# Delta rule in an encoder kernel: group norm and splits on another engine, key tiles of one chunk

## Chip, cores and metric

The kernel runs on one core of a Trainium2 chip. The metric is the device time of one execution in microseconds (us). Engines are called as in the profile: PE (TensorE matmuls) and PEld (its weight loads), DVE (VectorE), ACT (ScalarE), POOL (GpSimd), SP (SyncE, which here only issues DMAs).

## The reference

Two encoder layers over 1040 tokens (16 meta tokens and 1024 tokens) of width 1024. Each layer has an input projection, four heads of latent attention, eight heads of a generalised delta rule that runs once forward and once backward over the tokens, an output projection with a layer norm, and a mixture of 32 experts. The change lies in the delta rule and in the output projection beside it:

```
sa = einsum('bhvk,bhk->bhv', S, kk_t)                       # one step of the scan
S  = S * w_t - sa * b_t + v_t * k_t ;  y_t = S r_t
...
y  = y_f + y_b                                              # both directions
yn = (y - mean) * rsqrt(var + eps) * gn_g + gn_b            # group norm, 64 channels a head
out = (yn + bonus) * g
mixed = concat([y_att, out]) @ w_out
```

The kernel does the scan in chunks of 64 tokens: inside a chunk a triangular system is solved with matrices, and a state of 64x64 a head goes from chunk to chunk.

## The kernel before, in words

Function `rwkv` holds the delta rule of a layer. 17 chunks and two directions give 34 steps (33 in the last layer), taken in turn: a step forward, a step backward. Two steps make a **job**. Four stages are called for a job, and the main loop (at the end of `rwkv`) calls them for different jobs: `chain` of job j, `levels` of job j+1, `grams` of job j+3, `blocks` of jobs j+2 and j+3 together every second time.

- `grams` (L1498) loads the keys of a job into tile `T` (SP, L1512) and their partners into `BK` (L1514, L1517), multiplies them (L1528, tile `e`), masks the result into the other half of `T` (DVE, L1533) and into `AA` (ACT L1534, POOL L1540), scales `BK` (ACT, L1543) and transposes it into `BT` (L1547, L1548).
- `blocks` (L1551) solves 16x16 blocks: three multiplications on POOL (L1560 to L1562) and then 45 short DVE instructions one behind the other (L1569 to L1571).
- `levels` (L1580) makes the inverses `Y` of 64x64 from these (PE L1597, L1602, L1611, L1618; POOL L1589; DVE L1587, L1603, L1604; ACT).
- `chain` (L1638) carries the state. For each step: `tu` = `T`·`ring` (L1659), ACT copies it (L1661), `tu` = `Y`·t (L1677), ACT writes it into `ring` (L1678, L1679), `st` = `BT`·`ring` (L1683), DVE adds the decayed state `sp` from POOL (L1673) and writes the next step's `ring` (L1686). The outputs go to PSUM tile `y` (L1666, L1690) and from there into `yt` (DVE L1693 or ACT L1695).
- `finish` (L1703) follows when both directions of a tile of 128 tokens are done, from the middle of the stage on: statistics on DVE and POOL (L1708 to L1716), loads of the bonus and the gate into `bg` (SP, L1718, L1719), transposes on PE into a PSUM bank (L1727), then scale and shift out of PSUM on ACT, four times 128 columns (L1730), and on POOL one addition of the bonus (L1731) and one multiplication by the gate (L1732) over 512 columns.
- `attended` (L950) is a generator that the main loop advances once or twice a job. It does the output projection in between: it splits activations into a high and a low part (`split`, L204: ACT writes the high one at L209, the low one is a subtraction at L212, here on POOL), and multiplies each tile in three matmuls (L201 to L203). First the attention's half (tile `yraw`), then the delta rule's (tile `yTr`) as `finish` delivers it.

Buffers: `T` lives in two pools, used by pairs of jobs, with two buffers each and a job (8 units of 2x128 columns) in a buffer; so four jobs of `T` are on the chip and a load for job j+3 goes into the buffer of job j-1. `BK` has two buffers, `ring` six, PSUM tiles `e` and `y` two each, `bg` one.

What sets the order: nothing is ordered by hand. The framework puts the instructions of every engine, and the DMAs of SP, in one order by its own estimate of when each could start, and each engine then takes them strictly in that order. So a change of an instruction or of a buffer's size also moves others.

Of the kernel before, what the change touches and what calls it, by code (L numbers as in the profile page):

```python
# [11 lines left out]
F32 = mybir.dt.float32  # L12
# [158 lines left out]
def hybrid_encoder(ctx: ExitStack, tc: tile.TileContext, I, out):  # L171
# [184 lines left out]
    for li in range(DEPTH):  # L356
# [594 lines left out]
        def attended(bank):  # L951


            for kc in range(4):
                w_out(kc)
            yield
            for i, n, col in TILES[:nt]:
                raw = fp.tile([128, 4, 128], F32, name="yraw")
                nc.sync.dma_start(raw[:, :, :n], yatt_d[:, :, col:col + n].rearrange("a p t -> p a t"))
                ya = pair(fp, [128, 4, 128], "ya")  # L960
                split(ya[:, :, :n], raw[:, :, :n], None, nc.gpsimd)
                ht = fp.tile([128, D], F32, name="ht", bufs=2)
                nc.sync.dma_start(ht[:n], h_rows[2 * li][row0(i):row0(i) + n])
                for j in range(2):
                    js = slice(j * 512, (j + 1) * 512)
                    ps = bank()
                    for kc in range(4):
                        mm3(ps[:n], ya[:, kc, :n], wo[kc][:, js], start=kc == 0, stop=kc == 3)
                    nc.vector.scalar_tensor_tensor(ht[:n, js], ht[:n, js], ALPHA, ps[:n], op0=OP.mult, op1=OP.add)
                    if j == 1:  # L970
                        nc.sync.dma_start(a_d[row0(i):row0(i) + n], ht[:n])
                    yield
            for kc in range(4, 8):
                w_out(kc)
            yield

            while True:
                if not ready:
                    yield
                    continue  # L980
                i = ready.pop(0)
                _, n, col = TILES[i]
                ya = pair(fp, [128, 4, 128], "ya")
                split(ya[:, :, :n], yTr[:, :, col:col + n], None, nc.gpsimd)
                ht = fp.tile([128, D], F32, name="ht", bufs=2)
                nc.sync.dma_start(ht[:n], a_d[row0(i):row0(i) + n])
                for j in range(2):
                    js = slice(j * 512, (j + 1) * 512)
                    ps = bank()
                    for kc in range(4):  # L990
                        mm3(ps[:n], ya[:, kc, :n], wo[4 + kc][:, js], start=kc == 0, stop=kc == 3)
                    nc.vector.scalar_tensor_tensor(ht[:n, js], ht[:n, js], 1.0, ps[:n], op0=OP.mult, op1=OP.add,
                                                   accum_out=sums[:n, i, j:j + 1])
                    if j == 1:
                        nc.sync.dma_start(a_d[row0(i):row0(i) + n], ht[:n])
                        done.append(i)
                    yield
# [470 lines left out]
def rwkv(tc, li, last, K, P, pc, kr_d, bk_d, bon_d, g_dram, vt_d, yT, mhalf, kept, side, ready):  # L1468
# [29 lines left out]
    def grams(runs, sv):  # L1498
# [1 line left out]

        U = 4 * sum(n for _, _, n in runs)

        T = sv[0].tile([128, U, 2, 128], F32, name="T")
        BK = kb.tile([128, U, 2, 64], F32, name="BK")

        at, u0 = [], 0
        for d, c0, n in runs:
            us = slice(u0, u0 + 4 * n)
            at += [(d, c0 + u // 4, u % 4) for u in range(4 * n)]
            u0 += 4 * n  # L1510
            for o, h in enumerate(HALF):
                nc.sync.dma_start(T[h, us, o], kr_d[d, h, c0:c0 + n].rearrange("p c i x -> p (c i) x"))  # L1512
            cs = bk_d[d, :, c0:c0 + n].rearrange("p c i (a t) -> p (c i) a t", a=2)
            nc.sync.dma_start(BK[lo, us], cs[lo])  # L1514
            for a in range(2):

                nc.sync.dma_start(BK[hi, us, 1 - a], cs[hi, :, a])  # L1517
        AA = sv[1].tile([128, U, 128], F32, name="AA")
        A, AR = AA[:, :, :64], AA[:, :, 64:]
        BT = sv[1].tile([128, U, 2, 64], F32, name="BT")  # L1520


        for q0 in range(0, U, 4):
            q = slice(q0, q0 + 4)
            ps = [pe.tile([128, 4, 128], F32, name="e") for _ in HALF]
            for u in range(4):
                for o, h in enumerate(HALF):
                    nc.tensor.matmul(ps[o][:, u], BK[h, q0 + u].rearrange("p a t -> p (a t)"), T[h, q0 + u, o],  # L1528
                                     start=True, stop=True)
            mask = K(f"mask{at[q0][0]}")  # L1530
            for o in range(2):
                a, b = HALF[o], HALF[1 - o]
                V.tensor_tensor(T[b, q, o], ps[o][b], mask[b, None, :].to_broadcast([64, 4, 128]), op=OP.mult)  # L1533
                nc.scalar.activation(AA[a, q], ps[o][a], AF.Copy)  # L1534
        u0 = 0
        for d, c0, n in runs:
# [7 lines left out]
        for q0 in range(0, U, 4):  # L1544
            ps = bank().rearrange("p (a b) -> p a b", a=4)
            for u in range(4):
                nc.tensor.transpose(ps[:, u], BK[:, q0 + u].rearrange("p a t -> p (a t)"), ident)  # L1547
            nc.scalar.activation(BT[:, q0:q0 + 4].rearrange("p u o x -> p u (o x)"), ps, AF.Copy)  # L1548
        return T, A, AR, BT, {x: u for u, x in enumerate(at)}

    def blocks(As, E):  # L1551
# [84 lines left out]
    shared = {}  # L1636

    def chain(job, s, Y):  # L1638
        T, _, AR, BT, units = s
        for d, c in job:  # L1640
            ring = rings.pop((d, c))
            x = steps.index((d, c))
            if x + AHEAD < len(steps):
# [5 lines left out]
            def un(i):  # L1649
                return units[d, c, i]  # L1650
# [5 lines left out]
            tu, ps = shared["tu"][:, x % 2], shared["st"][:, x % 2]  # L1656
            for i in range(4):
                for o in range(2):
                    nc.tensor.matmul(tu[HALF[o], i], T[:, un(i), o, 0:64], ring[:, i, o], start=True, stop=True)  # L1659
            t0 = ch.tile([128, 4, 64], F32, name="t0", bufs=2)  # L1660
            nc.scalar.activation(t0, tu, AF.Copy)  # L1661
            if want:
                py = pq.tile([128, 4, 64], F32, name="y", bufs=2)
                for i in range(4):
                    for o in range(2):
                        nc.tensor.matmul(py[HALF[o], i], T[:, un(i), o, 64:], ring[:, i, o], start=i == 0, stop=False,  # L1666
                                         skip_group_check=True)
            if more:
                nring = rings[d, orders[d][pos + 1]]
# [10 lines left out]
            if more:  # L1680
                for i in range(4):
                    for o in range(2):
                        nc.tensor.matmul(ps[HALF[o], i], BT[:, un(i), o], ring[:, i, o], start=True, stop=True)  # L1683
                for o in range(2):
                    a = HALF[o]
                    V.tensor_tensor(nring[a, :, o], ps[a], sp[a], op=OP.add)  # L1686
# [14 lines left out]
    def finish(cs, bank=bank):  # L1701
# [25 lines left out]
                        nc.tensor.matmul(ps[h, i, 64 * k:64 * k + 64], yt[h, c, i], ident[h, h], start=True, stop=True)  # L1727
        yn = yT[:, :, col:col + n]
        for i in range(4):
            nc.scalar.activation(yn[:, i], ps[:, i, :n], AF.Identity, bias=P("gnb", i), scale=P("gng", i))  # L1730
        nc.gpsimd.tensor_tensor(yn, yn, bg[:, 0, :, :n], op=OP.add)  # L1731
        nc.gpsimd.tensor_tensor(yn, yn, bg[:, 1, :, :n], op=OP.mult)  # L1732

    steps = [(d, orders[d][x]) for x in range(NC) for d in range(2) if x < len(orders[d])]
    cuts = [*range(0, len(steps), 2), len(steps)]
# [59 lines left out]
```

## Time and profile before

| what | value |
|---|---|
| three runs | 3145.37 us median, 3142.09 to 3153.57 |
| the profiled execution | 3157.96 us, span of its instructions 3156.2 us |
| PE busy | 2707.3 us, 86% of the span |
| PEld busy | 2209.1 us, 70% |
| DVE busy | 2165.3 us, 69% |
| ACT busy | 1650.5 us, 52% |
| POOL busy | 1050.7 us, 33% |
| mean granted TensorE clock | 0.888 of full speed |

The profiled execution is 12.6 us (0.4%) above the median of the runs. A row of the trace names the engine, the line of the kernel, the operation and the tiles (output<-inputs); "idle before" is the time in which the engine had nothing to do ahead of the instruction, and behind the arrow stands what ended it. The delta rule of the first layer lies from about 625 to 1130 us of the span, that of the second from about 2200 to 2715 us.

### The profile page before, as it was taken

The numbers are of one execution on the slowest core, as the hardware profiler recorded it, in microseconds if no ns is written. First come the engines' busy times: TensorE is split into PE (matmuls) and PEld (weight loads), VectorE is DVE, ScalarE is ACT, GpSimd is POOL, SyncE is SP. The second block draws the span as 40 slices with busy tenths as digits, with TensorE's granted clock in tenths as the row PEclk, the third lists the DMA queues.
The fourth block names the chain that finished last, engine by engine and source line by source line (L and its number), as shares of the span: only waits on it lengthen the run. The fifth ranks groups of instructions, "written<-read, shape, count | busy, mean of one in ns | idle before, by whom it ended". The sixth has DMA issues, their size and how long they took to land. (4 is left out here: it accounts for less than half of the span.)

```text
span 3156.2 us, 58039 instructions
## 1 busy us (share of the span) xinstructions
PE 2707.3 (86%) x22160; PEld 2209.1 (70%) x22160; DVE 2165.3 (69%) x4257; ACT 1650.5 (52%) x3604; POOL 1050.7 (33%) x1049
## 2 busy tenths in 40 slices
PE   5998799979999997999589997988799989799982
PEld 4888688768777775666388866877687777666661
DVE  7568655475766678989756756444667675789896
ACT  5434454444444447888543435434544453488882
POOL 3656211143334532121246631111433353321111
PEclk9999999978887897999789988998788879899996
DMA  5345610233322357999824465201433233699996
GB/s 175 97 137 185 205 48 21 75 93 102 94 68 78 108 198 259 358 360 352 303 91 137 155 194 186 65 21 51 107 108 101 69 93 100 214 333 356 352 347 244
DMA packets 342732, 523.77 MB, mean 166 GB/s; under 512 B 110732, under 2 KB 263308, under 8 KB 315808
## 3 DMA queue, kind: packets, MB, share of 16 engines
q1 hardware_dynamic: 234832, 399.11, 38.8%
q10 hardware_dynamic: 93280, 87.04, 8.1%
q0 software_dynamic: 14336, 33.84, 3.2%
q8 instruction: 176, 2.88, 0.4%
q14 instruction: 108, 0.88, 0.1%
HBM read 406.57 MB, written 129.84 MB: 170 GB/s over the span
## 5 line engine op out<-in xcount | busy, mean ns | idle before, releaser
L1221 DVE TENSOR_TENSOR w_lo<-raw,w_hi 128x512 fp32r<-128x512 f32 x768 | 481.7, 684 | 49.4 <-ACT w_hi L1217 49.1
L1217 ACT ACTIVATE w_hi<-raw 128x512 fp32r<-128x512 f32 x768 | 424.7, 625 | 71.0 <-DMA raw<-in_w_moe_dram 57.3
L201 PE MATMUL pj<-hT_hi,w_hi 128*128 128x352 f32 (+1 forms) x912 | 303.9, 334 | 3.0 <-ACT k L437 2.7
L202 PE MATMUL pj<-hT_lo,w_hi 128*128 128x352 f32 (+1 forms) x912 | 301.8, 331 | 2.8 <-DVE hT_lo L212 2.8
L203 PE MATMUL pj<-hT_hi,w_lo 128*128 128x352 f32 (+1 forms) x912 | 300.3, 330 | 0.0
L201 PE MATMUL ph<-w_hi,xT_hi 128*96 128x512 f32 x512 | 213.8, 418 | 3.9 <-ACT w_hi L1217 3.9
L202 PE MATMUL ph<-w_lo,xT_hi 128*96 128x512 f32 x512 | 206.0, 402 | 1.4 <-DVE w_lo L1221 1.4
L1458 POOL DMA_INDIRECT y_rows<-y,VS x64 | 59.9, 936 | 440.1 <-ACT y L1405 440.1
L1528 PE MATMUL e<-T,BK 64*128 64x128 f32 x1072 | 181.0, 352 | 28.5 <-DMA T<-kr_d 19.0
L203 PE MATMUL ph<-w_hi,xT_lo 128*96 128x512 f32 x512 | 205.3, 401 | 0.0
L212 DVE TENSOR_TENSOR pT_lo<-tr,pT_hi 128x512 fp32r<-128x512 f32 (+2 forms) x176 | 101.3, 592 | 130.1 <-ACT pT_hi L209 129.7
L201 PEld LDWEIGHTS pj<-hT_hi,w_hi 128*128 128x128 f32 x912 | 177.2, 195 | 13.3 <-issue 7.5
L1528 PEld LDWEIGHTS e<-T,BK 64*128 64x128 f32 x1072 | 152.7, 244 | 44.9 <-DMA T<-kr_d 15.6
L202 PEld LDWEIGHTS pj<-hT_lo,w_hi 128*128 128x128 f32 x912 | 176.8, 194 | 9.3 <-issue 4.9
L203 PEld LDWEIGHTS pj<-hT_hi,w_lo 128*128 128x128 f32 x912 | 176.4, 194 | 4.9 <-issue 4.3
L1533 DVE TENSOR_TENSOR T<-e,cc 64x512 f32<-64x512 f32 x134 | 92.2, 688 | 103.8 <-PE e L1528 101.2
L1673 POOL TENSOR_TENSOR sp<-ring,pc 64x256 f32<-64x256 f32 x126 | 84.7, 672 | 171.6 <-DVE ring L1686 150.8
L209 ACT ACTIVATE pT_hi<-tr 128x512 fp32r<-128x512 f32 (+2 forms) x176 | 87.0, 517 | 99.9 <-PE tr L873 98.3
L1277 POOL DMA_INDIRECT xs<-h_rows,XS x64 | 77.3, 1208 | 159.9 <-PE tp L1235 97.0
L1570 DVE TENSOR_TENSOR sb<-sb,dg 128x16 f32<-128x16 f32 (+8 forms) x270 | 106.5, 395 | 32.0 <-POOL dg L1562 24.8
L1540 POOL TENSOR_TENSOR AA<-AA,cc 128x256 f32<-128x256 f32 x67 | 52.0, 777 | 221.4 <-ACT AA L1534 161.8
L421 POOL TENSOR_SCALAR w_hi<-w_raw 128x1024 fp32r<-128x1024 f32 x34 | 102.3, 3010 | 59.4 <-PE pj L202 59.4
(422 smaller groups left out, 7678.3 us busy)
## 6 DMA issues: line engine op xcount, KB each, us to landing
raw<-in_w_moe_dram SPq DMA_DIRECT2D x192, 1024.0 KB
w_raw<-in_w_in_dram SPq DMA_DIRECT2D x38, 512.0 KB
T<-kr_d SPq DMA_DIRECT2D x134, 128.0 KB
ys<-y_rows SPq DMA_DIRECT2D x16, 1024.0 KB
a_d<-ht SPq DMA_DIRECT2D x25, 512.0 KB
h_rows<-h ACTq DMA_DIRECT2D x24, 512.0 KB
kr_d<-KR ACTq DMA_DIRECT2D x16, 576.0 KB
bk_d<-BK ACTq DMA_DIRECT2D x16, 576.0 KB
```

The costliest lines, as they stand in the source:

```text
L201: nc.tensor.matmul(o, a.hi, b.hi, start=start, stop=False)
L202: nc.tensor.matmul(o, a.hi, b.lo, start=False, stop=False)
L203: nc.tensor.matmul(o, a.lo, b.hi, start=False, stop=stop)
L209: hi = nc.scalar.activation(dst.hi, src, AF.Copy)
L212: return hi, e_lo.tensor_tensor(dst.lo, src, dst.hi.bitcast(F32), op=OP.subtract)
L421: nc.gpsimd.tensor_scalar(w.hi, wr, 1.0, None, op0=OP.mult)
L1217: nc.scalar.activation(w.hi[:, cs], raw[:, cs], AF.Copy)
L1221: V.tensor_tensor(w.lo[:, cs], raw[:, cs], w.hi[:, cs].bitcast(F32), op=OP.subtract)
L1528: nc.tensor.matmul(ps[o][:, u], BK[h, q0 + u].rearrange("p a t -> p (a t)"), T[h, q0 + u, o], start=True, stop=True)
L1533: V.tensor_tensor(T[b, q, o], ps[o][b], mask[b, None, :].to_broadcast([64, 4, 128]), op=OP.mult)
L1570: V.tensor_tensor(sb[:, :, cs], sb[:, :, cs], dg[:, :, t_:t_ + 1].to_broadcast([128, n, w]), op=OP.mult)
L1673: nc.gpsimd.tensor_tensor(sp[a], ring[a, :, o], pc[a, d, :, c:c + 1].to_broadcast([64, 4, 64]), op=OP.mult)
```

## The change

1. In `finish`, the scale by `gn_g` and the addition of the bonus are one DVE instruction for each 128 columns, which reads the sums from PSUM; the shift by `gn_b` and the multiplication by the gate are another. ACT's four instructions and POOL's two are gone.
2. In `attended`, the low part of the split of the activations is computed by DVE instead of POOL (the weights' split stays on POOL).
3. `T` holds one chunk of one direction (four units) with four buffers in each pool, and `BT` likewise. The bytes on the chip and the number of DMAs are the same.

```diff
-                split(ya[:, :, :n], raw[:, :, :n], None, nc.gpsimd)
+                split(ya[:, :, :n], raw[:, :, :n])
...
-                split(ya[:, :, :n], yTr[:, :, col:col + n], None, nc.gpsimd)
+                split(ya[:, :, :n], yTr[:, :, col:col + n])
...
-        T = sv[0].tile([128, U, 2, 128], F32, name="T")
+        T, BT = {}, {}
...
-            for o, h in enumerate(HALF):
-                nc.sync.dma_start(T[h, us, o], kr_d[d, h, c0:c0 + n].rearrange("p c i x -> p (c i) x"))
+            for c in range(c0, c0 + n):
+
+                T[d, c] = sv[0].tile([128, 4, 2, 128], F32, name="T", bufs=4)
+                for o, h in enumerate(HALF):
+                    nc.sync.dma_start(T[d, c][h, :, o], kr_d[d, h, c])
...
-        BT = sv[1].tile([128, U, 2, 64], F32, name="BT")
...
+            bt = BT[at[q0][:2]] = sv[1].tile([128, 4, 2, 64], F32, name="BT", bufs=4)
...
         for i in range(4):
-            nc.scalar.activation(yn[:, i], ps[:, i, :n], AF.Identity, bias=P("gnb", i), scale=P("gng", i))
-        nc.gpsimd.tensor_tensor(yn, yn, bg[:, 0, :, :n], op=OP.add)
-        nc.gpsimd.tensor_tensor(yn, yn, bg[:, 1, :, :n], op=OP.mult)
+            V.scalar_tensor_tensor(yn[:, i], ps[:, i, :n], P("gng", i), bg[:, 0, i, :n], op0=OP.mult, op1=OP.add)
+        for i in range(4):
+            V.scalar_tensor_tensor(yn[:, i], yn[:, i], P("gnb", i), bg[:, 1, i, :n], op0=OP.add, op1=OP.mult)
```

The instructions of the whole program: DVE gets 136 more in `finish` (128 of them of 128 columns, 8 of 16) and 28 splits (27 of 512 columns, one of 64), ACT loses 68, POOL loses 34 in `finish` and 28 splits. PE and SP have the same instructions as before, in another order. (The changed file's lines are 3 to 5 higher from `grams` on: L1528 is L1531 there, L1659 is L1664, L1677 is L1682, L1683 is L1688, L1686 is L1691, L1690 is L1695.)

The DMAs on SP's queue, in the middle of the first layer's stage, before:

```order
L1630 DMA ring<-vt_d 64x4x64 x2
L1512 DMA T<-kr_d 64x4x128 x4
L959 DMA yraw<-yatt_d 128x4x128
L963 DMA ht<-h_rows_103 128x1024
L1630 DMA ring<-vt_d 64x4x64 x2
```

and in the changed kernel:

```order
L1634 DMA ring<-vt_d 64x4x64 x2
L1515 DMA T<-kr_d 64x4x128 x2
L959 DMA yraw<-yatt_d 128x4x128
L963 DMA ht<-h_rows_103 128x1024
L1634 DMA ring<-vt_d 64x4x64 x2
L1515 DMA T<-kr_d 64x4x128 x2
```

The load of a job's keys came in one piece of four DMAs; now the first chunk's two come where the four were, and the second chunk's two behind the next load of `ring`.

PE around the second step of a job in the first layer, before (`tu<-t,Y` is a step's product with `Y`, `st` the new state, `e` the products of `grams` for a later job, `m<-X,AA` a part of `levels`):

```order
L1677 MATMUL tu<-t_6783,Y 64x64 x8
L1666 MATMUL y<-ring,T 64x64 x5
L1683 MATMUL st<-ring,BT 64x64
L1690 MATMUL y<-ring,AA 64x64
L1528 MATMUL e<-T,BK 128x128 x4
L1611 MATMUL m<-X,AA 32x32 x10
L1683 MATMUL st<-ring,BT 64x64 x7
```

and in the changed kernel:

```order
L1682 MATMUL tu<-t_6791,Y 64x64 x8
L1671 MATMUL y<-ring,T 64x64 x5
L1531 MATMUL e<-T,BK 128x128 x8
L1688 MATMUL st<-ring,BT 64x64
L1695 MATMUL y<-ring,AA 64x64
L1615 MATMUL m<-X,AA 32x32 x2
L1688 MATMUL st<-ring,BT 64x64 x7
```

The eight products of the first chunk's keys (4 of them behind the first `st` before, the rest later) now stand ahead of the second step's `st`. Leaving out one place with 40 at the start of the second layer, which both have, 49 such products stood between a step's `tu<-t,Y` and its `st`, in 12 places of the whole program; now 128 do, in 27 places.

DVE at one `finish` of the first layer, before (the scale, bonus and gate of `yTr` are on ACT and POOL):

```order
L1713 TENSOR_REDUCE gst<-gsq 128x8
L1571 TENSOR_TENSOR Y_10155<-Y_10155,sb 128x16x15
L1714 TENSOR_SCALAR gst<-gst 128x8
L1686 TENSOR_TENSOR ring<-st,sp 64x4x64 x2
L1577 TENSOR_TENSOR Y<-Y_10155,cc 128x512 x2
```

and in the changed kernel, at the same tile of attention outputs:

```order
L1735 SCALAR_TENSOR_TENSOR yTr<-m,cp,bg 128x128 x4
L1737 SCALAR_TENSOR_TENSOR yTr<-yTr,cp,bg 128x128 x4
L969 SCALAR_TENSOR_TENSOR ht<-ht,e 16x512
L212 TENSOR_TENSOR ya_lo<-yTr,ya_hi 128x512
L1691 TENSOR_TENSOR ring<-st,sp 64x4x64 x2
```

The eight new instructions and a split stand directly ahead of the additions that make the next `ring`.

## Rows read from the trace of the kernel before

**Rows 1.** Stretches: the two delta-rule stages without their starts; us busy (count), clock, DMA.
```profile
core 0: us, PE busy (x) PEld busy (x) DVE busy (x) ACT busy (x) POOL busy (x), PEclk, DMA share, GB/s
640.00:1120.00 480.00, 432.97 (x6067) 358.00 (x6068) 321.41 (x847) 210.58 (x485) 197.96 (x208) 0.80 0.33 94
2240.00:2720.00 480.00, 422.61 (x5942) 351.31 (x5943) 317.59 (x833) 208.53 (x481) 199.27 (x208) 0.82 0.37 110
```
**Rows 2.** PE's waits, 640 to 1120 us: total us, times, longest.
```profile
PE e L1528 <- DMA T<-kr_d: 9.2, 7, 2.8
PE e L1528 <- ACT AA L1534: 6.6, 8, 1.9
```
**Rows 3.** PE's waits, 2230 to 2720 us.
```profile
PE e L1528 <- DMA T<-kr_d: 9.7, 5, 2.2
PE y L1666 <- DVE yt L1693: 6.5, 2, 4.0
PE m L1611 <- DVE X L1604: 6.4, 6, 2.4
```
**Rows 4.** Timeline, second layer, SP and PE: start, us, engine, instruction, [idle before].
```profile
2570.58 1.91 SPq L1512 DMA_DIRECT2D T<-kr_d  x3
...
2574.06 1.26 PE L1528 MATMUL e<-T,BK 64*128 64x128 f32 x10 [2.20 <-DMA T<-kr_d]
...
2583.93 1.12 PE L1666 MATMUL y<-ring,T 128*64 128x64 f32 x16 [4.00 <-DVE yt L1693]
```
**Rows 5.** One stretch of 20 us behind it; columns as in Rows 1.
```profile
2580.00:2600.00 20.00, 13.03 (x182) 11.28 (x184) 14.17 (x38) 8.68 (x21) 6.95 (x7) 0.57 0.06 16
```
**Rows 6.** Instructions removed or moved: count, duration in ns min/median/max, first and last start.
```profile
L1730 ACT ACTIVATE yTr<-m,cp x56: 447/457/466, 965.3 to 2698.0; 128x128 f32<-128x128 f32 x56
L1731 POOL TENSOR_TENSOR yTr<-yTr,bg x17: 326/1281/2048, 966.9 to 2711.3; 128x512 f32<-128x512 f32 x16, 128x64 f32<-128x64 f32 x1
L1732 POOL TENSOR_TENSOR yTr<-yTr,bg x17: 320/1282/2156, 968.2 to 2712.7; 128x512 f32<-128x512 f32 x16, 128x64 f32<-128x64 f32 x1
...
L212 POOL TENSOR_TENSOR ya_lo<-yraw,ya_hi x17: 322/1272/1279, 683.5 to 2488.6; 128x512 fp32r<-128x512 f32 x16, 128x64 fp32r<-128x64 f32 x1
L212 POOL TENSOR_TENSOR ya_lo<-yTr,ya_hi x11: 1265/1277/1726, 1026.5 to 2679.5; 128x512 fp32r<-128x512 f32 x11
```
**Rows 7.** The like on DVE: a split, and an instruction of 128 columns with two inputs.
```profile
L212 DVE TENSOR_TENSOR yr_lo<-yTr,yr_hi x8: 218/680/693, 1122.4 to 2716.7; 128x512 fp32r<-128x512 f32 x7, 128x64 fp32r<-128x64 f32 x1
...
L1562 DVE TENSOR_TENSOR dg<-tmp x2: 283/288/292, 643.9 to 2225.1; 128x128 f32<-128x128 f32 x2
```
**Rows 8.** Groups by line, DVE, 640 to 1120 us: busy us, mean ns, idle before.
```profile
L1571 DVE TENSOR_TENSOR Y<-Y,sb 128x16 f32<-128x16 f32 (+9 forms) x135 | 54.3, 402 | 3.8
```
**Rows 9.** Timeline: DVE at L1710 alone, then beside a long POOL instruction; DVE at L1570 alone.
```profile
951.30 0.68 DVE L1710 TENSOR_TENSOR yt<-yt,gst 128x512 f32<-128x512 f32 x1
...
1023.96 2.57 POOL L212 TENSOR_TENSOR wo_lo<-ht,wo_hi 128x1024 fp32r<-128x1024 f32 x1
...
1024.24 2.84 DVE L1710 TENSOR_TENSOR yt<-yt,gst 128x512 f32<-128x512 f32 x1
...
2576.17 0.29 DVE L1570 TENSOR_TENSOR sb<-sb,dg 128x128 f32<-128x128 f32 x1
```
**Rows 10.** Timeline, first layer: POOL without a gap, and DVE behind it.
```profile
1026.50 1.73 POOL L212 TENSOR_TENSOR ya_lo<-yTr,ya_hi 128x512 fp32r<-128x512 f32 x1
...
1031.17 1.53 POOL L1731 TENSOR_TENSOR yTr<-yTr,bg 128x512 f32<-128x512 f32 x1
...
1048.23 0.19 DVE L1570 TENSOR_TENSOR sb<-sb,dg 128x16 f32<-128x16 f32 x1 [1.09 <-POOL dg L1562]
```
**Rows 11.** Timeline, end of the first layer's stage: two layer-norm instructions, and POOL beside them.
```profile
1134.91 3.52 DVE L228 SCALAR_TENSOR_TENSOR h<-hres,ln_st,l1b 128x1024 f32<-128x1024 f32 x2
...
1135.30 2.05 POOL L1731 TENSOR_TENSOR yTr<-yTr,bg 128x512 f32<-128x512 f32 x1
1137.42 2.16 POOL L1732 TENSOR_TENSOR yTr<-yTr,bg 128x512 f32<-128x512 f32 x1
```

More of the change, by code (lines that the diff above doesn't have):

```diff
@@ L1525, in grams @@
             ps = [pe.tile([128, 4, 128], F32, name="e") for _ in HALF]
+            Tq = T[at[q0][:2]]
             for u in range(4):
                 for o, h in enumerate(HALF):
-                    nc.tensor.matmul(ps[o][:, u], BK[h, q0 + u].rearrange("p a t -> p (a t)"), T[h, q0 + u, o],
+                    nc.tensor.matmul(ps[o][:, u], BK[h, q0 + u].rearrange("p a t -> p (a t)"), Tq[h, u, o],
                                      start=True, stop=True)
@@ L1532, in grams @@
                 a, b = HALF[o], HALF[1 - o]
-                V.tensor_tensor(T[b, q, o], ps[o][b], mask[b, None, :].to_broadcast([64, 4, 128]), op=OP.mult)
+                V.tensor_tensor(Tq[b, :, o], ps[o][b], mask[b, None, :].to_broadcast([64, 4, 128]), op=OP.mult)
                 nc.scalar.activation(AA[a, q], ps[o][a], AF.Copy)
@@ L1547, in grams @@
                 nc.tensor.transpose(ps[:, u], BK[:, q0 + u].rearrange("p a t -> p (a t)"), ident)
-            nc.scalar.activation(BT[:, q0:q0 + 4].rearrange("p u o x -> p u (o x)"), ps, AF.Copy)
+            bt = BT[at[q0][:2]] = sv[1].tile([128, 4, 2, 64], F32, name="BT", bufs=4)
+            nc.scalar.activation(bt.rearrange("p u o x -> p u (o x)"), ps, AF.Copy)
         return T, A, AR, BT, {x: u for u, x in enumerate(at)}
@@ L1638, in chain @@
     def chain(job, s, Y):
-        T, _, AR, BT, units = s
+        Ts, _, AR, BTs, units = s
         for d, c in job:
+            T, BT = Ts[d, c], BTs[d, c]
             ring = rings.pop((d, c))
@@ L1658, in chain @@
                 for o in range(2):
-                    nc.tensor.matmul(tu[HALF[o], i], T[:, un(i), o, 0:64], ring[:, i, o], start=True, stop=True)
+                    nc.tensor.matmul(tu[HALF[o], i], T[:, i, o, 0:64], ring[:, i, o], start=True, stop=True)
             t0 = ch.tile([128, 4, 64], F32, name="t0", bufs=2)
@@ L1665, in chain @@
                     for o in range(2):
-                        nc.tensor.matmul(py[HALF[o], i], T[:, un(i), o, 64:], ring[:, i, o], start=i == 0, stop=False,
+                        nc.tensor.matmul(py[HALF[o], i], T[:, i, o, 64:], ring[:, i, o], start=i == 0, stop=False,
                                          skip_group_check=True)
@@ L1682, in chain @@
                     for o in range(2):
-                        nc.tensor.matmul(ps[HALF[o], i], BT[:, un(i), o], ring[:, i, o], start=True, stop=True)
+                        nc.tensor.matmul(ps[HALF[o], i], BT[:, i, o], ring[:, i, o], start=True, stop=True)
                 for o in range(2):
```

## The prediction

> **What bounds the kernel now.** I read the busy time by stretches first, since only the delta rule's two stages are touched: 960 of 3156 us. In both, PE counts as busy for nine tenths of the time, but at a granted clock of 0.80 and 0.82 of full speed [rows 1]. So the stage is not at PE's peak: PE's order is a chain of short products with ACT and DVE between them, and where PE stands still the clock falls too. DVE is busy for 321 and 318 of the 480 us, POOL for 198 and 199, ACT for about 210 [rows 1]. Next I read PE's own waits, because in a stage bound by PE's order only they and the clock can be won. Keys that have not landed stand first: 9.2 us in seven waits in the first layer, 9.7 us in five in the second [rows 2, 3]. Behind these come waits for ACT (6.6 us, [rows 2]) and for DVE (6.5 and 6.4 us, [rows 3]). No wait of PE is ended by POOL in this list; POOL matters by what it does to DVE and by a place where it runs without a gap.
>
> **Keys in tiles of one chunk.** The load for job j+3 goes into the buffer of job j-1. As one tile it is free only when both steps of that job are done; as two tiles the first chunk's half is free a step earlier. The order shows that: the block of four DMAs becomes two and two, with `ring` between. The reader sees the price of the block in one place: the DMAs are issued at 2570.58 us, and PE stands for 2.20 us until 2574.06 us [rows 4]. Half of each load comes a step earlier, so I take off half of the 18.9 us of waits: **-9.5 us**; the ends are 0 (the second half waits as long as all did) and -18.9 (none is left). That place also shows what follows: after the 2.20 us and a second wait of 4.00 us [rows 4], the clock over the next 20 us is 0.57 and PE is busy for 13.03 us [rows 5]. At full clock this work takes 13.03 x 0.57 = 7.4 us. I count one such place: **-5.6 us**, say -6. Bounds for the clock in general: a hundredth of it over the 855.6 us of PE's busy time in both stages [rows 1] is 855.6 x 0.01 / 0.81 = 10.6 us. The new order could move it by two hundredths either way, so plus or minus 21 us.
>
> **Off POOL.** 34 instructions in `finish` (32 of 1.28 us, two of 0.32) and 28 splits (27 of 1.27, one of 0.32) go [rows 6]: 41.6 + 34.6 = about 76 us of POOL's 397. Nearly all of it was beside other work, since POOL idles for over half of the stage. On the path I put one place: in the first layer POOL runs without a gap from 1026 to 1048 us, with a split of 1.73, an addition of 1.53 and a multiplication of 1.28 us among the work [rows 6, 10], and behind it DVE waits for `blocks` [rows 10]. **-4.5 us**; ends 0 and -4.5, as DVE's own wait there was only 1.09 us and PE had other products.
>
> **Off ACT.** 64 instructions of 0.457 us and four shorter ones are 31 us of ACT's 419 [rows 1, 6]. What of ACT's time shows up as PE standing still: 6.6 of 210.6 us [rows 1, 2], or 3%. 3% of 31 us is **-1 us**; ends 0 and -31.
>
> **Onto DVE.** 27 splits of 0.68 us and 128 instructions of 128 columns with two inputs at 0.288 us [rows 7], the nine small ones at 0.2 us: 18.4 + 36.9 + 1.8 = 57 us. No row shows this form reading PSUM; `finish` takes a scalar and two tensors, and the nearest row is one with two tensors of the same size. Something comes back, because POOL slows DVE: the same L1710 takes 0.68 us alone and 2.84 us beside a POOL instruction of 2.57 us [rows 9]. Over the stage: L1571 has a mean of 402 ns [rows 8], while a middle size alone takes 0.29 us [rows 9]. That is 0.112 x 135 = 15 us of a layer, and its twin L1570, as many and of the same shapes, doubles it: 30 us for 198 us of POOL. The 76 us that POOL loses are then worth 11.5 us, and DVE's load grows by 57 - 11.5 = 46 us, from 639 to 685. Of DVE's time 6.5 + 6.4 us in 317.6 show up as PE standing still [rows 1, 3], 4%: **+2 us**. The lower end is -11.5 (only the relief counts), the upper end +57 (all of it on the path).
>
> The Trainium skill ("SBUF — State Buffer", § Who interferes with whom) says that DVE and GpSimd lock a shared port pair for a whole instruction, and that a DVE instruction takes part if it has two inputs in SBUF. The row of 2.84 us agrees. By this rule alone relief could be as much as the overlap, 76 us times DVE's busy share, some 50 us instead of 11.5, and DVE's term 0 instead of +2. The rule also speaks against a part of the change: the splits and the second instruction of each pair have two inputs in SBUF and enter the lock themselves, against the POOL work that stays. I leave the sum as the rows give it.
>
> **The stage's end.** The last tiles' `finish` runs beside the layer norm. POOL's two instructions take 2.05 and 2.16 us there, against 1.28 us elsewhere [rows 6, 11], and DVE's two beside them take 3.52 us together [rows 11]. With the pair on DVE (8 x 0.288 = 2.3 us) in place of 4.2 us on POOL I take 2 us off in each layer: **-4 us**; ends 0 and -5.
>
> **Sum**: -9.5 - 6 - 4.5 - 1 + 2 - 4 = -23 us. Against the profiled execution's 3158 us that is 3135; it is 12.6 us above the median of the runs, so against the median, which is what will be measured, 3145.4 - 23 = **3122 us**. About 0.5% (15.7 us) is what a measurement of this kernel can tell from no change.
>
> **Rivals.**
> - *The waits only move* (hidden anyway). The stage is a chain of in-order engines; keys that land earlier meet the next wait, on ACT or DVE, a microsecond later. For it: each T wait is short, and PE is busy for nine tenths. Against: 18.9 us is the largest item in PE's list. Then all terms are near 0: 3145 us.
> - *The clock rises.* For it: the clock of 0.57 stands right behind two waits of PE [rows 4, 5], so every wait that goes may give more than itself. Three hundredths more over both stages are 32 us: 3122 - 32 = 3090 us. Against it: a new order makes new waits, and the clock may as well fall.
> - *Products ahead of the state* (slower). In the new order 128 products of `grams` instead of 49 stand between a step's product with `Y` and its `st`, in 27 places instead of 12. PE takes them strictly in order, so if the first chunk's keys, now loaded just ahead of them, land late, the wait falls on the chain itself. Price: 27 waits of up to the 2.20 us seen [rows 4] are 59 us, in place of the 18.9 us of now; with the other four terms (-7.5 us) that is 3145 - 7.5 + 59 - 19 = 3178 us. It decides from the point where the keys land later than PE reaches the products; against it, in the trace only 12 waits for keys lie in 26 such loads, and half are loaded a step earlier than now.
> - *DVE becomes the bound* (slower). The new instructions stand ahead of the additions to `ring`; at 2583.93 us PE already waited 4.00 us because DVE was late [rows 4]. If the whole 46 us lie on the path and the other terms, without DVE's, hold (-25): 3145 + 46 - 25 = 3166 us. It decides where the products for `st` are done before DVE comes to the addition. Against it: DVE idles for a third of both stages.
>
> **How the numbers follow.** Forecast (3105 to 3140): 0.40. Waits only move: 0.24. Clock rises: 0.15. Products ahead of the state: 0.13. DVE the bound: 0.08. Faster by over 0.5% (below 3129.6) are three quarters and more of the forecast's cases, all of the clock's and a few of the moved waits': 0.32 + 0.15 + 0.02 = 0.49. Slower by over 0.5% (above 3161.1) are most of the two slower rivals: 0.19. Within 0.5%: 0.32. The range, 3088 to 3174 us, reaches from the clock's case to between the two slower ones and leaves out 2 in 10: the far ends of both.
>
> **What would show it.** Right: PE's waits for the keys fall from 18.9 us to about half; the two stages' POOL time falls by some 70 us and DVE's rises by 40 to 50; L1570, L1571 and L1710 get shorter; the layer norm's pair takes less than 3.52 us; both stages together are some 20 us shorter, and all other stages are as long as before. Wrong: waits for keys ahead of `st` that are as long as before or longer; a granted clock below 0.80 in the stages; waits of PE for the additions to `ring` and to `yt` of over 20 us (DVE the bound); or another stage's time moving by more than a few microseconds.

## The result, and the profile of the changed kernel

| kernel | median | runs | ratio to before |
|---|---|---|---|
| before | 3148.13 us | 3142.09 to 3153.57 (4) | 1 |
| changed | **3109.51 us** | 3103.86 to 3114.61 (4) | **0.9888**, 95% interval 0.9856 to 0.992 |

The change is worth 38.6 us between the medians, 1.1% by the ratio. The profiled execution of the changed kernel took 3103.86 us, 54.1 less than the one of before; 9.8 + 5.7 us of that are where the two profiled executions lie against the medians of the table. A second set of runs of the changed kernel, beside other kernels and with before on the same chip, gave 0.9887 (0.9846 to 0.9928).

The stretches of [rows 1], in the changed kernel:

```profile
core 0: us, PE busy (x) PEld busy (x) DVE busy (x) ACT busy (x) POOL busy (x), PEclk, DMA share, GB/s
640.00:1120.00 480.00, 421.44 (x6268) 347.10 (x6267) 361.39 (x977) 213.73 (x491) 174.12 (x188) 0.88 0.38 108
2240.00:2720.00 480.00, 419.08 (x5985) 345.69 (x5984) 352.72 (x1017) 211.24 (x496) 151.76 (x167) 0.87 0.39 119
```

The clock is 0.88 and 0.87 where it was 0.80 and 0.82. These windows now reach past the stage, so from here on a stage is cut where the chain begins and ends: from the first to the last copy of `t` by ACT (L1661, now L1666). Before:

```profile
670.20:1118.40 448.20, 412.60 (x5892) 340.00 (x5888) 297.67 (x775) 196.62 (x458) 182.37 (x191) 0.81 0.33 95
2256.20:2688.70 432.50, 395.91 (x5720) 329.19 (x5718) 283.25 (x760) 190.13 (x445) 176.12 (x186) 0.82 0.34 98
```

and changed:

```profile
675.00:1085.80 410.80, 369.21 (x5923) 304.45 (x5920) 311.75 (x843) 184.72 (x434) 150.02 (x165) 0.90 0.35 99
2220.30:2626.90 406.60, 369.43 (x5719) 305.99 (x5718) 296.12 (x824) 180.26 (x422) 140.69 (x160) 0.88 0.36 102
```

Such a row can be split into three parts: PE's idle time (length minus busy), the **loss to the clock** (busy x (1 - PEclk)) and the rest, which is the same work at full clock. Both stages together:

| | length | PE idle | loss to the clock | work at full clock |
|---|---|---|---|---|
| before | 880.7 | 72.2 | 149.7 | 658.9 |
| changed | 817.4 | 78.8 | 81.3 | 657.4 |

The work is the same, as it must be. PE stands still as long as before, 7 us longer even. In this pair of profiles the clock accounts for all of the 63 us of the two stages (PEclk is printed to two decimals, which leaves each loss open by some 4 us either way). The pair lies far apart, though: the mean granted clock of the whole execution is 0.888 and 0.908 in these two, but 0.893 on average over 27 executions of before and 0.899 over five of the changed kernel in the second set. So the table shows which kind of time went, and more of it than an ordinary pair of executions would. Of PE's waits, those for the keys, the largest item of [rows 2, 3] in each layer behind the wait for the first `ring` (10.4 and 17.7 us), are gone. PE's waits in the changed kernel, layer 1 (from 600 to 1130 us; columns as in [rows 2]):

```profile
PE tu L1664 <- DMA ring<-vt_d: 10.7, 1, 10.7
PE e L1531 <- ACT AA L1537: 6.4, 7, 2.0
PE m L1615 <- DVE X L1608: 5.5, 4, 2.6
PE st L1688 <- ACT ring L1683: 5.4, 5, 3.3
PE e L201 <- ACT AA L1537: 5.2, 5, 1.5
PE y L1671 <- DVE yt L1698: 5.1, 4, 3.0
```

and layer 2 (2150 to 2720 us):

```profile
PE tu L1664 <- DMA ring<-vt_d: 17.3, 1, 17.3
PE m L1615 <- DVE X L1608: 11.6, 4, 6.3
PE y L1671 <- DVE yt L1698: 9.8, 3, 6.7
...
PE e L1531 <- ACT AA L1537: 5.3, 7, 1.4
```

No row "T<-kr_d" is left, in either layer. In its place PE waits for DVE's `X` (11.6 us where [rows 3] has 6.4), for `yt` (9.8 for 6.5) and for ACT's `AA` and `ring`. The rest of the kernel did not stand quite still: from the first expert product of layer 1 to the first copy of `t` in layer 2 it takes 1042.9 us instead of 1050.8 (1043.7 in the second profile of the changed kernel).

DVE's rows that the change adds or that get shorter, over the whole kernel (columns: instructions | busy us, mean ns of one | idle before). Two of before:

```profile
L1571 DVE TENSOR_TENSOR Y<-Y,sb 128x16 f32<-128x16 f32 (+8 forms) x270 | 108.1, 401 | 7.5
L1570 DVE TENSOR_TENSOR sb<-sb,dg 128x16 f32<-128x16 f32 (+8 forms) x270 | 106.5, 395 | 32.0 <-POOL dg L1562 24.8
```

and of the changed kernel, where these two are L1575 and L1574:

```profile
L1574 DVE TENSOR_TENSOR sb<-sb,dg 128x16 f32<-128x16 f32 (+8 forms) x270 | 101.5, 376 | 20.7 <-POOL dg L1566 13.5
L1575 DVE TENSOR_TENSOR Y<-Y,sb 128x16 f32<-128x16 f32 (+8 forms) x270 | 97.6, 362 | 7.4
L1737 DVE SCALAR_TENSOR_TENSOR yTr<-yTr,cp,bg 128x128 f32<-128x128 f32 (+1 forms) x68 | 28.6, 476 | 0.1
L1735 DVE SCALAR_TENSOR_TENSOR yTr<-m,cp,bg 128x128 f32<-128x128 f32 x56 | 15.8, 344 | 22.8 <-PE m L1732 22.8
L212 DVE TENSOR_TENSOR ya_lo<-yraw,ya_hi 128x512 fp32r<-128x512 f32 (+1 forms) x17 | 11.9, 702 | 6.2 <-ACT ya_hi L209 6.2
L1715 DVE TENSOR_TENSOR yt<-yt,gst 128x512 f32<-128x512 f32 (+1 forms) x17 | 11.4, 671 | 0.3
```

With 9.0 us for the eleven splits of `yTr` and 2.9 us for the twelve L1735 at the stage's end, 68.2 us come onto DVE. Its busy time rises from 2165.3 to 2196.7 us only, by 31.4; POOL's falls from 1050.7 to 970.7, ACT's from 1650.5 to 1621.6.

### The profile page after: what moved, and what is told of

The parts are those of the page before. It is cut to its first block, busy times and chain, and to the rows that moved or that the text cites. A ratio compares the mean times of both kernels' runs of the same rounds, so it can differ in the third digit from the quotient of the medians.

```text
span 3102.0 us, 58102 instructions
## 1 busy us (share of the span) xinstructions
PE 2640.3 (85%) x22160; PEld 2152.1 (69%) x22160; DVE 2196.7 (71%) x4421; ACT 1621.6 (52%) x3536; POOL 970.7 (31%) x987
## 5 line engine op out<-in xcount | busy, mean ns | idle before, releaser
L1221 DVE TENSOR_TENSOR w_lo<-raw,w_hi 128x512 fp32r<-128x512 f32 x768 | 482.1, 684 | 48.7 <-ACT w_hi L1217 47.5
L1531 PE MATMUL e<-T,BK 64*128 64x128 f32 x1072 | 152.3, 316 | 13.3 <-ACT AA L1537 11.7
L1531 PEld LDWEIGHTS e<-T,BK 64*128 64x128 f32 x1072 | 126.6, 211 | 28.2 <-ACT AA L1537 15.2
L1277 POOL DMA_INDIRECT xs<-h_rows,XS x64 | 76.2, 1191 | 160.9 <-PE tp L1235 89.1
L226 POOL TENSOR_TENSOR ln_st<-ln_st,mhalf 128x1 f32<-128x1 f32 (+1 forms) x43 | 66.1, 1538 | 168.6 <-DVE ln_st L225 152.7
L201 PE MATMUL o<-pT_hi,V_hi 128*128 128x256 f32 (+3 forms) x288 | 95.2, 331 | 26.7 <-ACT yatt L881 26.7
```

What stands on the lines that cost most here:

```text
L201: nc.tensor.matmul(o, a.hi, b.hi, start=start, stop=False)
L1221: V.tensor_tensor(w.lo[:, cs], raw[:, cs], w.hi[:, cs].bitcast(F32), op=OP.subtract)
L1277: return nc.gpsimd.indirect_dma_start(out=x, out_offset=None, in_=src[:], in_offset=bass.IndirectOffsetOnAxis(ap=xi, axis=0), bounds_check ...
```

## The experiments

Two theories stood against each other after the result: the parts act by what they take away (keys that come late, POOL and ACT), or the framework's new order of all engines carries the gain and the parts are the occasion. Each kernel was timed against before on the same chip; the ratio is to that.

**The parts alone.** Each kernel is before with some of the diff's hunks and nothing else.

Key tiles of one chunk (the hunks in `grams` and `chain`):

> Only the key tiles of one chunk (T and BT per chunk); the splits and the group norm stay where they were. Theory A, the key tiles carry the gain: PE's waits of the e products for T (18.9 us over both layers before, none in the changed kernel) are gone here too, the granted clock of the two stages rises from .80 and .82 to .86 or more, and the time is 3105 to 3122 us (ratio .987 to .992). Theory B, the moves from POOL and ACT to DVE carry it: the key waits go, but the clock stays near .81 to .83 and the time is 3130 to 3148 us. Theory C, the parts are worth what the prediction gave them (keys 15.5 of 23 us): scaled to the measured 39 us, some 26 us here, 3122 us, with the clock about two thirds of the way up.

Both moves to DVE (the hunks in `attended` and `finish`):

> Only the moves to DVE (the group norm's sums from PSUM and the splits of ya); keys in whole-job tiles as before. Theory A: the waits for T stay (some 15 to 19 us over both layers), the clock stays at .80 to .83, the time is 3138 to 3150 us. Theory B: most of the gain is here, 3105 to 3125 us, with the clock at .86 or more though the key waits stay. Theory C: some 13 us, 3135 us. In every theory POOL's busy time falls by about 76 to 80 us and DVE's rises by 30 to 50.

Only the hunk in `finish`:

> Only the group norm's affine part and its sums on DVE, with operands taken from PSUM; splits on POOL, keys in whole-job tiles. Theory A: 3138 to 3155 us. Theory B: half or more of what both moves bring. As the eight instructions of 128 columns took 343 ns each in the changed kernel and not 288, DVE's busy time should rise by some 45 us less relief from POOL; ACT's falls by some 29 us. If the end of the stage is what the DVE copies lengthen (last step to first expert product +5 us in the changed kernel), that stretch is 83 us in layer 1 and 70 in layer 2 here too.

Only the two hunks in `attended`:

> Only the splits of ya on DVE instead of POOL (28 of 1.28 us off POOL, .68 us on DVE); group norm and keys as before. Theory A: 3138 to 3150 us, within half a per cent of before. Theory B: the split ahead of the output product is half a microsecond shorter in 28 places and POOL is 36 us freer; at most 15 us, 3133 us. If the end of the stage is lengthened by the group norm alone, the last step to the first expert product is 76 to 78 us in layer 1 here, as before or shorter.

| kernel | ratio (95% interval) | key waits, both layers | PE idle | loss to the clock | work |
|---|---|---|---|---|---|
| key tiles | 0.9936 (0.9913 to 0.9958) | 0 | 91.4 | 106.1 | 651.6 |
| both moves | 0.9966 (0.9939 to 0.9993) | 11.7 | 85.4 | 98.4 | 659.1 |
| norm only | 1.0066 (1.0028 to 1.0104) | 23.0 | 96.3 | 144.1 | 656.8 |
| splits only | 1.0013 (0.9988 to 1.0037) | 14.0 | 79.0 | 107.6 | 661.4 |

The key tiles bring 20 us and both moves 11: by size this is theory C, the shares that the prediction gave them. The clock of the stages rises with either part alone (to 0.86 and 0.86, and to 0.88 and 0.86), where theories A and B each expected it to stay low with one of them. But the two halves of the moves don't add up: the norm alone costs 21 us, the splits alone nothing, both together gain. A sum of separate effects on the engines does not give that. The row of the splits alone also shows what a loss read from one profile is worth: it is 42 us below that of before, and the time is the same. POOL's busy time is as expected in all of them: 1048.9 us with the key tiles, which take nothing off it, and 971.2, 1005.1 and 1013.1 in the other three. That the norm lengthens the stage's end is not shown either: the stretch from the last copy of `t` to the first split of an expert weight on DVE (L1221, 8 to 10 us ahead of the first expert product itself) is 81.1 us in layer 1 with the norm alone and 84.0 with the splits alone.

**A new order and nothing else.**

```diff
-            for o, h in enumerate(HALF):
+            for o, h in reversed(list(enumerate(HALF))):
                 nc.sync.dma_start(T[h, us, o], kr_d[d, h, c0:c0 + n].rearrange("p c i x -> p (c i) x"))
```

> The kernel before, with the two key loads of a run issued in the other order (upper half first): nothing is added or moved between engines, but the framework's order of all engines is drawn anew. Theory O, a new order alone moves the time by as much as the parts of the change did: at least 8 us from before, either way. Theory P, the parts act by what they take from an engine or free in a buffer: within 5 us of before (3143 to 3153 us), with the key waits at 15 to 22 us over both layers. In both theories the decomposition should hold: stage time = work at full clock (668 to 680 us for both stages in the six kernels so far) + PE's idle time + half of the time at the lower clock level.

Measured: 3137.54 us where before took 3163.52 on this chip, ratio **0.9922** (0.9892 to 0.9953). No work moved, no buffer changed, and 25 us are gone: as much as the key tiles bring (20 us), within the two intervals. Its stages:

```profile
674.40:1102.40 428.00, 379.28 (x5890) 311.09 (x5887) 295.99 (x775) 193.12 (x459) 181.88 (x191) 0.87 0.35 99
2236.70:2651.30 414.60, 361.88 (x5718) 299.21 (x5718) 276.86 (x759) 187.36 (x445) 174.48 (x186) 0.89 0.35 101
```

PE idle 101.4 us, loss to the clock 89.1, work 652.0. Two of its waits, layer 1 and layer 2:

```profile
PE e L1528 <- DMA T<-kr_d: 1.1, 2, 0.8
...
PE e L1528 <- DMA T<-kr_d: 1.3, 2, 0.9
```

So the waits for keys, 18.9 us before, can go with whole-job tiles too. A new order alone moves the time by more than the 8 us that theory O asks for. It does not rule theory P out: that forecast holds only while the key waits stay at 15 to 22 us, and they fell to 2.4. Over the five kernels with whole-job tiles the ratio even goes nearly in step with the key waits: 0.9922 at 2.4 us, 0.9966 at 11.7, 1.0013 at 14.0, 1 at 18.9, 1.0066 at 23.0, about 2 us of time for each us of waits. Whether late keys cost that much, or whatever else an order brings makes both, no run separates.

**Keys held back.** The changed kernel with `name="T", bufs=3` instead of 4:

> The changed kernel with three instead of four buffers for the key tiles of one chunk: a key load has to wait for a step that comes later. Theory P: waits for keys come back (over 10 us in both layers together, none before), the time at the lower clock level rises from 218 us towards 280 or more, and the time is 3125 to 3145 us. Theory O: the time is anywhere from 3100 to 3150 us and bears no relation to the key waits.

Measured: 3445.6 us, ratio 1.0894 (1.0858 to 1.0931), outside of both theories. The first stage:

```profile
677.70:1257.70 580.00, 443.76 (x5982) 369.70 (x5978) 297.81 (x837) 189.97 (x443) 144.20 (x167) 0.74 0.25 70
```

Over both stages PE idles 279.9 us and loses 226.9 to the clock. Of its waits in layer 1, PE's and SP's queue:

```profile
PE m L1601 <- DVE X L1591: 45.8, 7, 10.8
PE e L1531 <- DMA T<-kr_d: 22.0, 8, 3.1
...
SPq L1634 <- PE y L1695: 186.1, 23, 26.5
```

Keys are late again (45.2 us in both layers), but the larger part is elsewhere: SP waits 186.1 us to load the next steps' `ring` (29.6 in the changed kernel) and PE waits for the inverse. Which of the two comes first is not settled. What the fourth buffer saves is far more than the waits that name the keys.

**The start of the stage filled.** In the main function, behind the first `ring` tiles of the changed kernel (the products are not read by anyone):

```diff
                 new_ring(*steps[x])
+            for _ in range(2):
+                pf = bank()
+                for x in range(6):
+                    nc.tensor.matmul(pf.rearrange("p (a b) -> p a b", a=8), ident, gs[0][1], start=True, stop=True)
```

> The changed kernel with twelve products of 128x512 (identity times the first job's AA, into a bank that nobody reads) in PE's queue just ahead of the first product with the state, where PE waits 10.7 us in layer 1 and 17.3 in layer 2 and the clock is at its lower level for some 40 us of the next 45. Theory C, PE's standing still is paid for through the clock: the fill keeps the level up, about half of 40 us comes back in each layer, less up to 3 us where the fill is longer than the wait: 3075 to 3100 us. Rival: the low level there has another cause (the short dependent products behind the wait), the stretches stay, and the time is 3108 to 3125 us.

Measured: ratio 0.9929 (0.9903 to 0.9955), so no gain over 0.9888; applied to before's 3148 us it is 3126 us, just above both ranges. Layer 1 from 655 to 700 us, the changed kernel and then the filled one:

```profile
655.00:700.00 45.00, 27.26 (x228) 23.73 (x228) 33.02 (x85) 17.96 (x37) 26.85 (x27) 0.55 0.52 138
```

```profile
655.00:700.00 45.00, 32.77 (x286) 23.48 (x285) 31.02 (x70) 18.12 (x40) 24.26 (x26) 0.73 0.52 135
```

The lift of the clock is there: the wait for `ring` falls from 10.7 to 3.1 us and the clock rises from 0.55 to 0.73. The gain is not: the first copy of `t` comes at 686.4 us, not earlier than the 675.0 and 680.9 us of the two profiles of the changed kernel. ACT's rows show what it stands behind, in the changed kernel and then in the filled one:

```profile
674.02 1.06 ACT L209 ACTIVATE wo_hi<-ht 128x1024 fp32r<-128x1024 f32 x1 [12.61 <-DMA ht<-in_w_out_dram]
674.98 0.37 ACT L1666 ACTIVATE t<-tu 128x256 f32<-128x256 f32 x1
```

```profile
684.66 0.63 ACT L209 ACTIVATE ya_hi<-yraw 128x512 fp32r<-128x512 f32 x1 [4.05 <-DMA yraw<-yatt_d]
685.20 1.26 ACT L1546 ACTIVATE BK<-BK,pc 128x128 f32<-128x128 f32 x4
686.36 0.36 ACT L1666 ACTIVATE t<-tu 128x256 f32<-128x256 f32 x1
```

In both, PE's sixteen products for `tu` are done a microsecond or two (at 673.0 and 682.6 us) before ACT leaves its wait for a load of the output projection, and the copy comes behind that. So in layer 1 PE's pace does not set that time; in layer 2 of the changed kernel the copy waits 0.9 us for PE. The fill also drew a new order: ten of the sixteen products run at 669.95 us, and the other six come from 681.90 us on, behind products of `grams` and `levels` for which PE waits 2.35 and 4.00 us. What the lifted clock would be worth in the old order, and behind this place, the run does not show.

**The stage's end.** The changed kernel, but the tiles that are finished after the last step keep ACT and POOL:

```diff
+        if at_end:
+            for i in range(4):
+                nc.scalar.activation(yn[:, i], ps[:, i, :n], AF.Identity, bias=P("gnb", i), scale=P("gng", i))
+            nc.gpsimd.tensor_tensor(yn, yn, bg[:, 0, :, :n], op=OP.add)
+            nc.gpsimd.tensor_tensor(yn, yn, bg[:, 1, :, :n], op=OP.mult)
+        else:
...
```

> The changed kernel, but the tiles that are finished after the last step, beside the layer norm, keep ACT's scale and shift and POOL's addition and multiplication. If DVE's eight instructions there are what makes the stretch from the last step to the first expert product 83.5 and 70.1 us long (78.3 and 65.3 before), it falls by some 5 us in each layer: 3100 us. If it is the splits and the order, it stays: 3105 to 3115 us. By theory O the order of both stages is drawn anew too, and the time may move by 10 us or more either way.

Measured: 0.9898 (0.9862 to 0.9935), the changed kernel's ratio. The stretch from the last copy of `t` to L1221 is 85.6 and 68.1 us, as in the changed kernel (83.5 and 70.1): DVE's instructions there are not what lengthens it.

**Where the wide products lie.** Three more kernels test whether the clock follows the 128x512 products of `attended` that stand between the chain's short ones; the changed kernel runs beside them.

> The changed kernel once more, as it stands, as the anchor for the three runs beside it. Every theory: the ratio to before is .985 to .992. Its granted clock in the two stages is .86 to .89 and the time lost to the clock (PE's busy time, each microsecond weighted with what the granted clock lacks to full speed) about 84 us over both stages, as in the first profile of it (before: 160).

```diff
-        for _ in range(2 if j < 5 else 1):
+        for _ in range(1 + (j % 2 == 0)):
```

> The changed kernel with the output projection's generator advanced twice in every other job and once in the others, instead of twice in the first five jobs and once after that: the 128x512 products lie more evenly. Theory W, the clock of a stretch follows how much 128x512 work lies in it: in the eighths of the stage that hold 28 or more us of it the clock takes 0 to 7 us, in those that hold under 16 it takes 7 to 14 (before). An even spread then loses less: 60 to 80 us instead of 84, and the time is 10 to 25 us below the changed kernel beside it. Theory O, it is a new order and no more: within 15 us of it, either way.

```diff
             stage(k, x)
-        for _ in range(2 if j < 5 else 1):
-            next(side)
+            if k == 3 or (k == 0 and j < 5):
+                next(side)
```

> The changed kernel with the generator advanced as often as before, but between the stages of a job (behind the chain and behind the key products) instead of behind all four: the number per job is the same, only the emission order differs. Theory W: little changes in how the 128x512 work is spread over the stage, so within 6 us of the changed kernel beside it. Theory O: 10 us or more away from it, either way, though nothing is added, removed or moved to another engine.

```diff
-        for _ in range(2 if j < 5 else 1):
+        for _ in range(4 if j < 5 else 1):
```

> The changed kernel with the generator advanced four times instead of twice in the first five jobs: the attention's half of the output projection is done by the fifth job, and the middle of each stage has no 128x512 work until the first tiles are finished. The work is the same. Theory W: the middle of each stage (some 100 us) falls to the lower clock level for most of its time, the loss to the clock rises by 20 to 50 us in all, and the time is 20 to 60 us above the changed kernel beside it. Theory O or a stage bound by its waits: within 15 us of it.

| kernel | ratio (95% interval) | PE idle | loss to the clock | work |
|---|---|---|---|---|
| changed, again | 0.9887 (0.9846 to 0.9928) | 74.4 | 101.8 | 652.3 |
| every other job twice | 0.9982 (0.9951 to 1.0012) | 90.8 | 91.3 | 669.3 |
| between the stages of a job | 0.9947 (0.9924 to 0.9971) | 91.5 | 90.1 | 660.7 |
| four in the first five jobs | 1.0046 (1.0022 to 1.007) | 116.7 | 127.4 | 644.0 |

The changed kernel again has its ratio, but a loss of 101.8 us where some 84 were expected. The bunched kernel went as theory W has it, 1.6% (45 us) above the changed one, with 26 us more loss. Its middle, where no 128x512 product is left (855 to 975 us), and the same stretch of the changed kernel (second profile, 860 to 980):

```profile
855.00:915.00 60.00, 47.56 (x818) 41.08 (x816) 39.28 (x127) 25.89 (x64) 18.16 (x24) 0.77 0.25 66
915.00:975.00 60.00, 40.97 (x706) 35.11 (x706) 39.15 (x116) 22.63 (x55) 16.91 (x22) 0.72 0.20 52
```

```profile
860.00:920.00 60.00, 56.13 (x1034) 47.52 (x1034) 43.32 (x116) 31.99 (x77) 24.10 (x30) 0.97 0.33 90
920.00:980.00 60.00, 50.10 (x836) 40.69 (x834) 57.07 (x171) 23.93 (x57) 21.04 (x23) 0.86 0.33 90
```

Without wide products both PE's busy time and the clock fall. But spreading them more evenly than the changed kernel does lost 0.95% (20 us between the medians) instead of gaining, more than the 15 us that theory O allowed as well; and mere placing between the stages of a job lost 0.6% (13 us), as theory O has it. Theory W holds for taking the wide products away, and fails as a way to gain. No kernel tried was faster than the changed one.

**What follows from all.** Put in two sets, with and without key tiles of one chunk, and without the three kernels that hold keys back, add products or bunch them:

| keys | ratios | mean | key waits |
|---|---|---|---|
| whole job | 1, 0.9966, 1.0066, 1.0013, 0.9922 | 0.9993 | 18.9, 11.7, 23.0, 14.0, 2.4 |
| one chunk | 0.9936, 0.9888, 0.9898, 0.9982, 0.9947 | 0.9930 | 0, 0, 0.6, 0, 0 |

The sets lie 0.6% apart, 20 us; inside each, kernels that differ by a detail lie 0.9 to 1.4% apart. The key tiles take the key waits away in every order that was drawn. That they are worth some 20 us is likely, and no more than that: five draws a set with such a spread don't settle it. The sets also differ in the moves to DVE, which four of the five kernels below have; above, one has both and two have one of them. Within each set that makes little difference: 0.9929 on average with both moves against 0.9936 with neither below, 0.9966 against 0.9961 above. What the moves to DVE are worth by themselves is within the draw, and stays open.

## Why the prediction came out right, and where its steps were wrong

The forecast, 3105 to 3140 us, holds the measured 3109.5; the time named, 3122, is 12.5 us too high. The sum, -23 us, stands against -38.6.

- **Keys, -9.5 us.** The waits went from 18.9 us to 0, the far end of the term and not half. (They were not the largest item of PE's list, as the prediction has it: the wait for the first `ring` takes 10.4 and 17.7 us.) As waits they gave nothing, though: PE's idle time went from 72.2 to 78.8 us. In this the rival "the waits only move" was right: the next waits, for `X`, `yt`, `AA`, took their place. If they paid, it was through the clock.
- **Clock, -6 us (bounds 21 either way).** The step that failed, in its size. It was sized by one place, the 13.03 us of work at 0.57 behind a wait [rows 5], and bounded by two hundredths of the clock. The clock of the two stages rose by nine and six hundredths in the pair of profiles, and by six and four with the second profile of the changed kernel (0.87 and 0.86); the loss to the clock fell by 149.7 - 81.3 = 68.4 us, and by 48 with the second profile (101.8). Both are more than the 38.6 us between the medians (the profiled execution of before lies 9.8 us above its median), and the splits alone have 42 us less loss without any gain. So the size of the term stays open within tens of us, and what raised the clock does too. The rival "the clock rises" named the mechanism and gave it 32 us and a chance of 0.15. The row that would have sized it was there: [rows 1] has 855.6 us of PE's busy time at 0.81, a loss of some 160 us against 18.9 us of key waits. The clock was the large item of the stage, and the prediction sized the gain by the small one.
- **Off POOL, -4.5 us.** POOL lost 80 us for 76 forecast. DVE's wait for POOL's `dg` in layer 1 fell from 9.1 to 1.3 us. No row shows that it reached PE.
- **Off ACT, -1 us.** 28.9 us left ACT, for 31; nothing to be seen on the path.
- **Onto DVE, +2 us.** The load was mis-sized twice. The new form takes 0.344 us and not 0.288, with a mean of 0.476 for the second of the pair, so 68.2 us came instead of 57. The relief was 68.2 - 31.4 = 36.8 us instead of 11.5: L1570 and L1571 together gave 15.5 over both layers, and L1577, L1709, L1710 and L228 another 12; the remaining 9 were not followed. Net 31 instead of 46. The rule of the Trainium skill ("SBUF — State Buffer", § Who interferes with whom) would have made the relief some 50 us by the prediction's estimate; the trace lies between, nearer to the rule than to the row that the prediction scaled. What the rule says against the change shows as well: the second instruction of the pair takes up to 1647 ns and a split of `ya` up to 2182 ns, for medians of 344 and 685, while the first, with one input in PSUM, never takes over 352 ns.
- **The stage's end, -4 us.** The step held where it was measured: no L228 beside the layer norm takes over 1.29 us any more (up to 2.33 before, its pair in [rows 11]). The stretch from the last copy of `t` to L1221 as a whole went the other way: 78.3 and 65.3 us became 83.5 and 70.1. The experiment with ACT and POOL there rules out the reason that lay near, and the cause stays open.
- **Rivals on the slower side.** Neither happened. No product waits for keys ahead of `st`; `st` waits for ACT's `ring`, 5.4 and 1.1 us. PE's waits for `yt` are 14.9 us in both layers, below the 20 that would have shown DVE as the bound.
- **What the working had no room for**: a term for the order itself. It stands only in the clock's bounds ("The new order could move it by two hundredths either way"), and the exchange of two loads shows that a new order alone can be worth 25 us. That the sum came near is in part luck: its terms named other items than those that moved, and with another order the same parts can lie within 0.5% of before, as the kernel with 0.9982 does. One of its signs of being wrong did show: the time between the two stages moved by 7.9 us.

## What to carry to other kernels

Split a stage bound by a chain of short products into idle time, loss to the clock and work before pricing single waits: here the loss to the clock was twice PE's idle time, and the two profiles differ in it alone. Take more than one profile of each kernel before pricing it: two profiles of the same kernel gave 81.3 and 101.8 us. Where a framework orders the engines by its own estimates, measure one edit first that moves no work (exchange two loads), and look at which waits it changed; differences below what that does (0.8% here) are not evidence for the reason that was meant. To see what a part is worth, compare means over several orders with and without it, not one kernel with one kernel.

## What the runs showed of the hardware

- DVE's form with a scalar and two tensors over 128 columns takes the same time from PSUM as from SBUF, 343 and 344 ns in the median:

```profile
L1735 DVE SCALAR_TENSOR_TENSOR yTr<-m,cp,bg x56: 330/343/352, 932.3 to 2636.1; 128x128 f32<-128x128 f32 x56
...
L1737 DVE SCALAR_TENSOR_TENSOR yTr<-yTr,cp,bg x68: 221/344/1647, 934.3 to 2652.8; 128x128 f32<-128x128 f32 x64, 128x16 f32<-128x16 f32 x4
```

  The Trainium skill ("Perfetto Trace Analysis", § Optimizing Scalar/DVE Operations) puts DVE's overhead at about 60 ns on SBUF and 125 on PSUM, by which the first would be some 65 ns longer (an estimate from that page). The two medians don't show such a difference. POOL's work beside the second does not hide it: the 39 of its 64 instructions of 128 columns with no POOL instruction beside them have a median of 344 ns too (332 to 348). In the first form only one of the two tensors lies in PSUM; no run has both there.
- Few waits of PE are no sign of a stage that goes well: the exchange of two loads has 29 us more idle time than before and 61 us less loss to the clock. That is no rule of exchange between the two: the norm alone has more of both (96.3 and 144.1) than the changed kernel (78.8 and 81.3).
- Filling 10 us of PE's wait with products of 128x512 lifted the clock from 655 to 700 us, the filled stretch included, from 0.55 to 0.73.
- The prediction has it that the clock falls where PE stands still. It also falls where PE does not: in the changed kernel PE is busy without a gap from 646 to 654 us at full clock, from 652.9 us on with eighteen products of one column, and then goes on, as busy, at the lower of the two levels (0.50, 1.2 GHz).

```profile
646.00:654.00 8.00, 8.00 (x62) 7.11 (x60) 6.95 (x25) 4.94 (x14) 1.97 (x2) 1.00 0.01 2
655.00:661.00 6.00, 5.97 (x24) 4.79 (x23) 5.00 (x17) 4.96 (x9) 5.79 (x4) 0.50 0.37 70
```
